# Time mixing of a two-layer encoder: chain and inverses as whole-array products with block-diagonal held operands

## The chip, the cores and the metric

The kernel runs on one core of a Trainium2 chip. A time is the device time of one execution in microseconds; a kernel's time is the median of its runs. All arithmetic is float32; the dense projections hold each operand as two rounded halves (`fp32r`) whose products are added.

## The reference

One sequence of 256 tokens, width 2048, 32 heads of 64, two layers. Layer 0 is RWKV-7 time mixing, layer 1 chunked attention; each is followed by a squared-ReLU MLP of width 8192, with norms and gates that a conditioning vector sets. The change touches the time mixing alone:

```python
def step(S, inp):                      # per head, S is 64 x 64, over 256 tokens
    r_t, w_t, k_t, v_t, kk_t, a_t = inp
    sa = jnp.einsum('bhvk,bhk->bhv', S, -kk_t)
    S = (S * w_t[:, :, None, :] + sa[..., None] * (kk_t * a_t)[:, :, None, :]
         + v_t[..., None] * k_t[:, :, None, :])
    y = jnp.einsum('bhvk,bhk->bhv', S, r_t)
    return S, y
...
y = ((y - mean) * lax.rsqrt(var + GN_EPS) * ln_w + ln_b)      # per head
y = y + jnp.sum(r_h * k_h * r_k, axis=-1, keepdims=True) * v_h
y = y.reshape(B, T, D).astype(h.dtype) * g
return y @ w_o
```

## The kernel before

The state is not stepped token by token. Tokens are taken in 4 chunks of 64; within a chunk the recurrence becomes matrix products with masked 64x64 Gram matrices and the inverse of a unit triangular one. Two heads form a pair, one on partitions 0 to 63, the other on 64 to 127; there are 16 pairs.

Each pair goes through four stages, and a software pipeline (`layer_a`) keeps one pair in each: the dense projections of `k` and `r` (`proj_steps`, 64 dense products at L405 and L406: 512 and 256 streamed columns), `early` (decays, norms, factors), `invert` and `late`. In each of 19 periods 16 slots are issued; in each slot some steps of `late`, `invert` and `early` and one part of the dense work. From this order a scheduler makes each engine's fixed queue. In the last three periods the output projection's first tiles (`o`, L394 to L396) take the dense part. In some slots a row of the conditioning weights is added up on VectorE (`acc`, L447), and its sums taken on TensorE (L469).

`invert` builds the Gram matrix of `bh` with `kr` (`gr`, L101), takes its diagonal 32x32 blocks, and inverts them by doubling: in each of 4 levels VectorE transposes `u` (L231), TensorE multiplies by the level's masked block (`iv<-tt,al`), ScalarE copies the result to `xs` (L235), TensorE multiplies `u` (`iv<-u,xs`) and VectorE adds (L246). A fifth level joins the two 32x32 halves (`co`). All these are 32x32 products in the array's four diagonal 32x32 tiles (`tiles`, L107): 16 for a level's half step, 4 chunks by 4 blocks. Masks of all levels are applied beforehand on GpSimd (`al`, L216).

`late` is the chain over the 4 chunks: for each, `g` (L273, L276), `sa` (L280), the state `zs` (L290, L292) and the output `py` (L283, L286, L301), each as two 64x64 products, one for each head, in the array's two diagonal 64x64 tiles. ScalarE copies `g` and `sa` out of PSUM, VectorE `zs`. The output is channel-major: its variance is a product of its squares with a block of ones (L111). Then come the gate's product (L315) and three operations on VectorE.

An f32 product is issued by the hardware as two passes, each with a load of its held operand, so it leaves two records under PE (the product) and two under PEld (the load).

Of the kernel before, what the change touches and what calls it, by code (L numbers as in the profile page):

```python
# [39 lines left out]
def _constants():  # L40
# [16 lines left out]
    for l in range(5):  # L57
        b = 1 << l
        m = ((i[:, None] // (2 * b) == i[None, :] // (2 * b))
             & (i[:, None] % (2 * b) >= b) & (i[None, :] % (2 * b) < b))  # L60
        put(f"lev{l}", np.tile(-m.T[:H, :H].astype(np.float32), (2, 1)))
    at["levs"] = (at["lev1"][0], 4 * H)
# [15 lines left out]
class Pair:  # L78
# [9 lines left out]
    def s(self, name="s", bufs=10):  # L88
        return self.b.pw.tile([P, T], F32, tag=name, bufs=bufs, name=name)

    def big(self, name, bufs):
        return self.b.pw.tile([P, 4, P], F32, tag=name, bufs=bufs, name=name)

    @staticmethod
    def ch(t):
        return t.rearrange("p (c t) -> p c t", t=C)
# [6 lines left out]
    def tiles(self, o, lhsT, rhs, pairs):  # L103

        for c in range(4):
            for R, K in pairs:
                self.b.nc.tensor.matmul(o[QS[K], c, :], lhsT[QS[R], c, :], rhs[QS[R], c, :], start=True, stop=True,  # L107
                                        tile_position=(H * R, H * K))
# [9 lines left out]
    def early(self):  # L118
# [37 lines left out]
        self.bh, self.kh = s("bh", 2), s("kh", 2)  # L156
# [8 lines left out]
        kr = self.kr = self.big("kr", 3)  # L165
        nc.vector.tensor_tensor(out=kr[:, :, 0:C], in0=ch(kk), in1=e0, op=ALU.mult)
        nc.vector.tensor_tensor(out=self.bh, in0=self.bh, in1=kk, op=ALU.mult)
        nc.vector.tensor_tensor(out=kr[:, :, C:P], in0=ch(r), in1=e1, op=ALU.mult)
# [3 lines left out]
        yield  # L172


        bk = self.bk = pw.tile([P, 3, 4, C], F32, tag="bk", bufs=3, name="bk")
        pt = b.psm().rearrange("p (a c k) -> p a c k", a=2, c=4)
        self.each(lambda c: pt[:, 0, c, :], lambda c: ch(v)[:, c, :], lambda c: cst("cen"))
        nc.scalar.copy(bk[:, 2], pt[:, 0])
        yield
        pbn = b.psm()[:, :T]  # L180
# [4 lines left out]
    def invert(self):  # L185
        b, nc, s, ch, kr, bk, bh, kh = self.b, self.b.nc, self.s, self.ch, self.kr, self.bk, self.bh, self.kh
        cst, pp = b.cst, b.pp

        def every(name):
            return cst(name).unsqueeze(1).to_broadcast([P, 4, H])  # L190

        def half(name, bufs):
            return b.pw.tile([P, 4, H], F32, tag=name, bufs=bufs, name=name)


        ui = cst("ui").unsqueeze(1).to_broadcast([P, 4, P])
        ts = []
        for src in (bh, kh):
            t = s()
            nc.gpsimd.tensor_tensor(out=ch(t), in0=ch(src), in1=self.pc.to_broadcast([P, 4, C]), op=ALU.mult)  # L200
            ts.append(t)
        pg = pp.tile([P, 4, P], F32, tag="gr", bufs=1, name="gr")
        self.each(lambda c: pg[:, c, :], lambda c: ch(bh)[:, c, :], lambda c: kr[:, c, :])
        ar = self.ar = s("ar", 2)
        nc.vector.tensor_tensor(out=ch(ar), in0=pg[:, :, C:P], in1=ui[:, :, C:P], op=ALU.mult)


        da, co, u = half("da", 2), half("co", 2), half("u", 2)
        for i, K in enumerate(QS):
            n = H * (i % 2)  # L210
            nc.scalar.copy(da[K], pg[K, :, n:n + H])
            if i % 2 == 0:
                nc.scalar.mul(co[K], pg[K, :, H:C], -1.0)
        nc.gpsimd.tensor_tensor(out=u, in0=da, in1=every("lev0"), op=ALU.mult)
        als = b.pw.tile([P, 4, 4, H], F32, tag="al", bufs=2, name="al")
        nc.gpsimd.tensor_tensor(out=als, in0=da.unsqueeze(1).to_broadcast([P, 4, 4, H]),  # L216
                                in1=cst("levs").rearrange("p (l k) -> p l k", l=4).unsqueeze(2).to_broadcast([P, 4, 4, H]),
                                op=ALU.mult)
        yield
        nc.vector.tensor_tensor(out=u, in0=u, in1=every("eye_h"), op=ALU.add)  # L220
# [4 lines left out]
        nc.scalar.copy(bk[:, 0:2], pt)  # L225
        yield
        uf = self.u = b.uf[self.j % 2]
        down, up = ((0, 1), (2, 3)), ((1, 0), (3, 2))
        for l in range(1, 6):
            tt_, xs = half("tt", 1), half("xs", 1)  # L230
            nc.vector.transpose(out=tt_.rearrange("p c t -> p (c t)"), in_=u.rearrange("p c t -> p (c t)"))  # L231
            pi = pp.tile([P, 16, H], F32, tag="iv", bufs=1, name="iv")[:, 0:4, :]
            if l < 5:
                self.tiles(pi, als[:, l - 1], tt_, [(i, i) for i in range(4)])
                nc.scalar.copy(xs, pi)  # L235
            else:
                self.tiles(pi, co, tt_, down)
                for i, K in enumerate(QS):
                    if i % 2:
                        nc.scalar.copy(xs[K], pi[K])  # L240
                    nc.gpsimd.tensor_copy(uf[K, :, H * (i % 2):H * (i % 2) + H], u[K])
            yield
            pi = pp.tile([P, 16, H], F32, tag="iv", bufs=1, name="iv")[:, 0:4, :]
            if l < 5:
                self.tiles(pi, xs, u, [(i, i) for i in range(4)])
                nc.vector.tensor_tensor(out=u, in0=u, in1=pi, op=ALU.add)  # L246
            else:
                self.tiles(pi, xs, u, up)
                for K in QS[::2]:
                    nc.vector.tensor_copy(uf[K, :, H:C], pi[K])  # L250
            if l == 2:
                pg = pp.tile([P, 4, P], F32, tag="gr", bufs=1, name="gr")
                self.each(lambda c: pg[:, c, :], lambda c: ch(kh)[:, c, :], lambda c: kr[:, c, :])
                mk = self.mk = self.big("mk", 2)
                nc.vector.tensor_tensor(out=mk, in0=pg, in1=ui, op=ALU.mult)
            yield

    def late(self):
        b, nc, j, s, ch, v = self.b, self.b.nc, self.j, self.s, self.ch, self.v
        kr, ar, mk, bk, u, pc, heads = self.kr, self.ar, self.mk, self.bk, self.u, self.pc, self.heads  # L260
        pw, pp = b.pw, b.pp

        pyt = pp.tile([P, 2, T], F32, tag="py", bufs=1, name="py")
        py = pyt[:, 0, :]
        zs = None
        for c in range(4):
# [5 lines left out]
            for K in heads:  # L272
                nc.tensor.matmul(pch[K, 0, :], mk[K, c, 0:C], bk[K, 2, c, :], start=True, stop=(c == 0))  # L273
            if c:
                for K in heads:
                    nc.tensor.matmul(pch[K, 0, :], kr[K, c, 0:C], zs[K, :], start=False, stop=True)  # L276
            nc.scalar.copy(g, pch[:, 0, :])
            yield
            for K in heads:
                nc.tensor.matmul(pch[K, 1, :], u[K, c, :], g[K, :], start=True, stop=True)  # L280
            nc.scalar.mul(sa, pch[:, 1, :], -1.0)
            for K in heads:
                nc.tensor.matmul(ch(py)[K, c, :], bk[K, 2, c, :], mk[K, c, C:P], start=True, stop=False)  # L283
            if c:
                for K in heads:
# [908 lines left out]
```

## Time and profile before

| | us |
|---|---|
| median of 3 runs | 2711.76 (2709.57 to 2712.15) |
| the profiled execution's own time | 2709.18 |
| its span, first to last instruction | 2707.4 |
| of it, the time mixing's pipeline | 210 to 750 |
| TensorE busy in these 540 us | 532.2 |
| VectorE, ScalarE, GpSimd busy there | 442.0, 270.2, 134.5 |

In a row of the profile "L107 PE MATMUL iv<-u,xs 32\*32 32x32 f32 x32" is line, engine, operation, output and operands by the program's names, the part of the array that is used (rows\*columns), the streamed operand (partitions x columns) and the number of records. In a timeline the first two numbers are start and length in microseconds. TensorE's products overlap: the length goes to the end of the last result, so what one costs is read from the distance between starts.

### The profile page before, as it was taken

How to read it: one execution, taken by the hardware profiler on the slowest of the kernel's cores; microseconds unless marked ns; L12 is line 12 of the kernel's file. 1: busy time of each engine (PE TensorE's matmuls, PEld its weight loads, DVE VectorE, ACT ScalarE, POOL GpSimd, SP SyncE). 2: the span in 40 equal slices, each digit the busy share in tenths (PEclk: the TensorE clock that was granted, in tenths of full speed). 3: DMA queues.
4: the chain of work that ended last, by engine and by line, in shares of the span. 5: the costliest groups of instructions: out<-in, count | busy, mean ns of one | idle time of the engine just before them, and what ended most of it. 6: DMA issues, size and time to landing. Idle time of an engine off the chain costs nothing.

```text
span 2707.4 us, 58382 instructions
## 1 busy us (share of the span) xinstructions
PE 2645.1 (98%) x23690; PEld 2236.3 (83%) x23690; DVE 2104.9 (78%) x3109; ACT 1347.8 (50%) x2432; POOL 214.9 (8%) x320
## 2 busy tenths in 40 slices
PE   6999999999999999999999999999999999999997
PEld 3777777777888888888888898877898888888886
DVE  5778888888788788888888898899987555555555
ACT  3346444555355536445355554465565464453553
POOL 0002222322110000000000100000100000000002
PEclk9999999999999999999999999999999999999999
DMA  9966655665587789988889769887867555555553
GB/s 338 313 227 207 203 191 180 191 195 177 184 280 264 255 324 329 330 307 319 322 316 329 252 220 316 322 287 252 288 193 259 188 188 186 187 188 186 189 188 120
DMA packets 217390, 662.64 MB, mean 245 GB/s; under 512 B 21408, under 2 KB 68896, under 8 KB 217120
## 3 DMA queue, kind: packets, MB, share of 16 engines
q1 hardware_dynamic: 215056, 656.36, 71.7%
q8 instruction: 186, 3.05, 0.4%
q10 hardware_dynamic: 2064, 2.54, 0.3%
q14 instruction: 84, 0.69, 0.1%
HBM read 656.72 MB, written 2.10 MB: 243 GB/s over the span
## 4 chain that ended last, share of the span: by engine, by line
PE 91%; DVE 3%; issue 3%; ACT 1%; DMA 1%; POOL 1%; DVEq 0%; ACTq 0%; SPq 0%; POOLq 0%
PE pj L405 47%; PE pj L406 23%; PE iv L107 2%; PE pj L395 2%; PE pj L396 2%; PE pj L394 2%; PE gr L101 1%; PE o L394 1%; PE ms L101 1%; PE chn L273 1%; PE chn L280 1%; PE ms L111 1%; PE py L315 1%; DVE wL L374 1%; PE o L395 0%
## 5 line engine op out<-in xcount | busy, mean ns | idle before, releaser
L374 DVE TENSOR_TENSOR wL<-raw,wH 128x1024 fp32r<-128x1024 f32 x772 | 941.8, 1220 | 353.5 <-ACT wH L371 348.8
L405 PE MATMUL pj<-aHL,wH 128*128 128x512 f32 x3328 | 1214.3, 405 | 2.0 <-DVE x L914 1.1
L371 ACT CAST wH<-raw 128x1024 fp32r<-128x1024 f32 x772 | 805.9, 1045 | 796.6 <-PE pj L405 650.4
L406 PE MATMUL pj<-aHL,wL 128*128 128x256 f32 x3328 | 938.8, 282 | 0.0
L405 PEld LDWEIGHTS pj<-aHL,wH 128*128 128x128 f32 x3328 | 628.0, 189 | 154.4 <-issue 11.4
L405 PE MATMUL pj<-hHL,wH 128*128 128x512 f32 x2048 | 722.4, 398 | 0.0
L406 PEld LDWEIGHTS pj<-aHL,wL 128*128 128x128 f32 x3328 | 628.3, 189 | 3.9 <-issue 0.8
L406 PE MATMUL pj<-hHL,wL 128*128 128x256 f32 x2048 | 574.4, 281 | 0.0
L405 PEld LDWEIGHTS pj<-hHL,wH 128*128 128x128 f32 x2048 | 384.5, 188 | 93.8 <-DVE hHL L960 0.2
L406 PEld LDWEIGHTS pj<-hHL,wL 128*128 128x128 f32 x2048 | 386.8, 189 | 0.5 <-DVE wL L374 0.3
L447 DVE SCALAR_TENSOR_TENSOR acc<-rada,ct,acc 128x1024 f32<-128x1024 f32 x255 | 326.3, 1280 | 11.7 <-DMA rada<-w_ada 11.1
L511 POOL TENSOR_TENSOR ss<-ss,sq 128x256 f32<-128x256 f32 x56 | 54.8, 979 | 1587.1 <-ACT sq L510 1586.9
L985 DVE SCALAR_TENSOR_TENSOR x<-pj,mod,x 128x256 f32<-128x256 f32 x256 | 123.4, 482 | 58.4 <-PE pj L406 54.6
L447 DVE SCALAR_TENSOR_TENSOR acc<-raw,ct,acc 128x1024 f32<-128x1024 f32 x105 | 135.6, 1291 | 3.8 <-DMA raw<-w_ada 3.7
L396 PE MATMUL pj<-aHL,wL 128*128 128x258 f32 x384 | 108.6, 283 | 1.6 <-DVE wL L374 1.6
L957 ACT ACTIVATE t<-t 128x256 f32<-128x256 f32 x112 | 46.8, 418 | 126.9 <-DVE t L929 126.9
L395 PE MATMUL pj<-aHL,wH 128*128 128x258 f32 x384 | 109.6, 286 | 0.0
L394 PE MATMUL pj<-aHL,wH 128*128 128x258 f32 x384 | 109.5, 285 | 0.0
L396 PEld LDWEIGHTS pj<-aHL,wL 128*128 128x128 f32 x384 | 73.9, 193 | 1.9 <-DVE wL L374 1.8
L395 PEld LDWEIGHTS pj<-aHL,wH 128*128 128x128 f32 x384 | 73.3, 191 | 0.1
L394 PEld LDWEIGHTS pj<-aHL,wH 128*128 128x128 f32 x384 | 73.0, 190 | 0.2
L959 ACT ACTIVATE t<-t 128x256 f32<-128x256 f32 x128 | 53.4, 417 | 3.4
(244 smaller groups left out, 2846.6 us busy)
## 6 DMA issues: line engine op xcount, KB each, us to landing
raw<-w_up SPq DMA_DIRECT2D x256, 512.0 KB, 4.3
raw<-w_down SPq DMA_DIRECT2D x256, 512.0 KB, 4.2
rada<-w_ada SPq DMA_DIRECT2D x208, 512.0 KB, 5.7
raw<-w_ada SPq DMA_DIRECT2D x112, 512.0 KB, 4.4
rawa<-w_ada SPq DMA_DIRECT2D x64, 512.0 KB, 6.7
rada<-w_ada_kv SPq DMA_DIRECT2D x64, 512.0 KB, 6.2
raw<-w_k SPq DMA_DIRECT2D x32, 512.0 KB, 4.7
raw<-w_r SPq DMA_DIRECT2D x32, 512.0 KB, 4.7
```

What stands on the lines that cost most here:

```text
L101: self.b.nc.tensor.matmul(o(c)[K], lhsT(c)[K], rhs(c)[K], start=True, stop=True)
L107: self.b.nc.tensor.matmul(o[QS[K], c, :], lhsT[QS[R], c, :], rhs[QS[R], c, :], start=True, stop=True, tile_position=(H * R, H * K))
L371: nc.scalar.copy(Hf, raw)
L374: eng.tensor_tensor(out=Lf, in0=raw, in1=Hf, op=ALU.subtract)
L394: nc.tensor.matmul(ps, H[:, i, :], a(kt)[:, 0, :], start=(first and kt == 0), stop=False)
L395: nc.tensor.matmul(ps, H[:, i, :], a(kt)[:, 1, :], start=False, stop=False)
L396: ins = nc.tensor.matmul(ps, L[:, i, :], a(kt)[:, 0, :], start=False, stop=(last and kt == KT - 1))
L405: nc.tensor.matmul(ps, H[:, i, :], a(kt), start=(kt == 0), stop=False)
L406: ins = nc.tensor.matmul(ps[:, 0, :], L[:, i, :], a(kt)[:, 0, :], start=False, stop=(kt == KT - 1))
L447: nc.vector.scalar_tensor_tensor(out=self.acc, in0=raw, scalar=ck, in1=self.acc, op0=ALU.mult, op1=ALU.add)
L511: (eng or nc.gpsimd).tensor_tensor(out=self.ss, in0=self.ss, in1=sq, op=ALU.add)
L985: nc.vector.scalar_tensor_tensor(out=x, in0=ps[:, i, :], scalar=self.mods[(layer, 5)][:, n:n + 1], in1=x, op0=ALU.mult, op1=ALU.add)
```

## The change

The 32x32 and 64x64 products of inverses and chain become products of the whole 128x128 array. Their held operands are 128x128 matrices with the heads' (or quarters') blocks on the diagonal and zeros elsewhere. These operands (`kr`, `nega`, `co`, `xs`, `xc`, `ar`, `uf`, `bk`, `mk`) live in buffers that are zeroed once and whose diagonal blocks alone are written: a copy or product into such a buffer is now one instruction for each head or quarter. Most of them have one buffer. `nega` holds the whole negative block; a level's mask is applied when the result is taken into `u`, by a predicated copy on VectorE. The sign is put into `bh`. The chain's output becomes token-major: squares are summed along the row on VectorE, the normed output `yn` is transposed back by TensorE with `eye`. The two transpositions of `bh` and `kh`, and the Gram matrix of `kh`, stand at the end of `invert` (12 steps in place of 13). The inverses' products go through the new function `whole`; transpositions and Gram matrices stay 64x64 products.

```diff
-    def tiles(self, o, lhsT, rhs, pairs):
+    @staticmethod
+    def of(h, t):
+        K = slice(C * h, C * h + C)
+        return t[K][..., K]
+
+    def whole(self, o, lhsT, rhs):
         for c in range(4):
-            for R, K in pairs:
-                self.b.nc.tensor.matmul(o[QS[K], c, :], lhsT[QS[R], c, :], rhs[QS[R], c, :], start=True, stop=True,
-                                        tile_position=(H * R, H * K))
+            self.b.nc.tensor.matmul(o[:, c, :], lhsT[:, c, :], rhs[:, c, :], start=True, stop=True)
...
-        kr = self.kr = self.big("kr", 3)
-        nc.vector.tensor_tensor(out=kr[:, :, 0:C], in0=ch(kk), in1=e0, op=ALU.mult)
-        nc.vector.tensor_tensor(out=kr[:, :, C:P], in0=ch(r), in1=e1, op=ALU.mult)
+        kr = self.kr = b.kr[j % 2]
+        for part, src, e in ((0, kk, e0), (1, r, e1)):
+            for h, K in enumerate(self.heads):
+                nc.vector.tensor_tensor(out=self.of(h, kr)[:, :, part, :], in0=ch(src)[K], in1=e[K], op=ALU.mult)
...
         for i, K in enumerate(QS):
             n = H * (i % 2)
-            nc.scalar.copy(da[K], pg[K, :, n:n + H])
+            nc.vector.copy_predicated(u[K], flips("lev0", K), pg[K, :, n:n + H])
+            nc.scalar.copy(nega[K, :, K], pg[K, :, n:n + H])
...
         for l in range(1, 6):
...
             if l < 5:
-                self.tiles(pi, als[:, l - 1], tt_, [(i, i) for i in range(4)])
-                nc.scalar.copy(xs, pi)
+                self.whole(pi, nega, tt_)
+                for K in QS:
+                    nc.scalar.copy(xs[K, :, K], pi[K])
             else:
-                self.tiles(pi, co, tt_, down)
+                self.whole(pi, co, tt_)
+                for i in (0, 2):
+                    nc.scalar.copy(xc[QS[i + 1], :, QS[i]], pi[QS[i + 1]])
...
             if l < 5:
-                self.tiles(pi, xs, u, [(i, i) for i in range(4)])
-                nc.vector.tensor_tensor(out=u, in0=u, in1=pi, op=ALU.add)
+                self.whole(pi, xs, u)
+                nc.vector.copy_predicated(u, flips(f"lev{l}"), pi)
             else:
-                self.tiles(pi, xs, u, up)
+                self.whole(pi, xc, u)
...
-            for K in heads:
-                nc.tensor.matmul(pch[K, 1, :], u[K, c, :], g[K, :], start=True, stop=True)
-            nc.scalar.mul(sa, pch[:, 1, :], -1.0)
-            for K in heads:
-                nc.tensor.matmul(ch(py)[K, c, :], bk[K, 2, c, :], mk[K, c, C:P], start=True, stop=False)
+            mm(pch[:, 1, :], u[:, c, :], g, start=True, stop=True)
+            nc.scalar.copy(sa, pch[:, 1, :])
+            mm(py[:, c, :], mk[:, c, 1, :], bv[:, c, :], start=True, stop=False)
...
-        self.head_sums(var, sq)
+        nc.vector.tensor_reduce(out=rg, in_=ch(sq), axis=AX.X, op=ALU.add)
...
+        nc.vector.tensor_tensor(out=yn, in0=py, in1=rg.unsqueeze(2).to_broadcast([P, 4, C]), op=ALU.mult)
+        yield
+        self.each(lambda c: yf[:, c, :], lambda c: yn[:, c, :], lambda c: b.cst("eye"))
...
+            def spread(name, *shape):
+                t = pw.tile([P, *shape, P], F32, name=name)
+                nc.gpsimd.memset(t, 0.0)
+                return t
+
+            self.kr = [spread(f"kr_{i}", 4, 2) for i in range(2)]
+            self.nega, self.co, self.xs, self.xc = (spread(n_, 4) for n_ in ("nega", "co", "xs", "xc"))
+            self.ar = [spread(f"ar_{i}", 4) for i in range(2)]
+            self.uf, self.bk, self.mk = spread("uf", 4), spread("bk", 2, 4), spread("mk", 4, 2)
```

In the changed kernel the dense lines 405 and 406 are 411 and 412, the inverses' products are L108, the grams L203, other 64x64 products L97, the chain's L285 to L306. How the change moves TensorE's queue is shown at two places. The first is one level of an inverse in the steady state; a shape here is the output's, so 32x32 is one tile and 128x32 the whole array. Before:

```order
L107 MATMUL iv<-tt,al 32x32 x16
L273 MATMUL chn<-bk,mk 64x64
L276 MATMUL chn<-zs,kr 64x64 x2
L405 MATMUL pj<-aHL,wH 128x512
L406 MATMUL pj<-aHL,wL 128x256
L405 MATMUL pj<-aHL,wH 128x512
L107 MATMUL iv<-u,xs 32x32 x16
```

With the change, one level in the steady state:

```order
L108 MATMUL iv<-tt,nega 128x32 x4
L411 MATMUL pj<-aHL,wH 128x512
L412 MATMUL pj<-aHL,wL 128x256
L411 MATMUL pj<-aHL,wH 128x512
L412 MATMUL pj<-aHL,wL 128x256
L203 MATMUL gr<-kr_2235,kh 64x128 x2
L108 MATMUL iv<-u,xs 128x32 x4
```

Sixteen products become four, and two of the eight products of the Gram matrix of `kh` have moved between the two halves of the step, where the chain's small products stood.

The second place is the chain on TensorE. Before, `g` is used, the state formed, and dense products follow each group:

```order
L280 MATMUL chn<-g,uf_2235 64x64 x2
L286 MATMUL py<-kr,zs 64x64 x2
L405 MATMUL pj<-aHL,wH 128x512
L406 MATMUL pj<-aHL,wL 128x256
L405 MATMUL pj<-aHL,wH 128x512
L406 MATMUL pj<-aHL,wL 128x256
L290 MATMUL chn<-bk 64x64 x2
L292 MATMUL chn<-sa,bk 64x64 x2
L301 MATMUL py<-ar,sa 64x64 x2
```

With the change, in the second chunk of the same kind of period:

```order
L292 MATMUL py<-bv,mk 128x64
L111 MATMUL ms<-sq,csts 128x256
L285 MATMUL chn<-bv,mk 128x64
L287 MATMUL chn<-zs,kr_2237 128x64
L294 MATMUL py<-zs,kr_2237 128x64
L290 MATMUL chn<-g,uf 128x64
L297 MATMUL chn<-bv,bk 128x64
L298 MATMUL chn<-sa,bk 128x64
L306 MATMUL py<-sa,ar_2249 128x64
```

Here a chunk's whole chain stands in one piece with no dense product in it; in its other chunks dense products stand between the groups as before. On ScalarE the copy after an inverse's product was one and is now four, with casts of weight halves between them. Before:

```order
L235 COPY xs<-iv 128x128
L277 COPY g<-chn 128x64
L371 CAST wH<-raw 128x1024
L281 ACTIVATE sa<-chn 128x64
L151 ACTIVATE s<-s 128x256
```

With the change:

```order
L239 COPY xs<-iv 32x4x32 x4
L848 COPY k<-pj 128x256
L377 CAST wH<-raw 128x1024
L288 COPY g<-chn 128x64
L291 COPY sa<-chn 128x64
```

Four quarter copies stand where one whole one stood, and the casts are queued between such groups in both.

More of the change, by code (lines that the diff above doesn't have):

```diff
@@ new lines, in half, with flips, gram @@
+        def half(name):
+            return b.pw.tile([P, 4, H], F32, tag=name, bufs=1, name=name)
+        def flips(name, K=slice(None)):
+            return every(name, K).bitcast(mybir.dt.uint32)
+        def gram(t):
+            pg = pp.tile([P, 4, P], F32, tag="gr", bufs=1, name="gr")
+            for c in range(4):
+                for h, K in enumerate(self.heads):
+                    nc.tensor.matmul(pg[K, c, :].rearrange("p (a t) -> p a t", t=C), ch(t)[K, c, :],
+                                     self.of(h, kr)[:, c, :, :], start=True, stop=True)
+            return pg
```

160 lines of the change are left out of this document (70 added, 90 removed).

## The prediction

> **What bounds the kernel now.** I read the page first, then the busy time of the stretch in which the changed code runs, then what TensorE waits for there, and last its timeline.
>
> ```profile
> span 2707.4 us, 58382 instructions
> PE 2645.1 (98%) x23690; PEld 2236.3 (83%) x23690; DVE 2104.9 (78%) x3109; ACT 1347.8 (50%) x2432; POOL 214.9 (8%) x320
> PE 91%; DVE 3%; issue 3%; ACT 1%; DMA 1%; POOL 1%; DVEq 0%; ACTq 0%; SPq 0%; POOLq 0%
> ```
>
> TensorE holds 91% of the chain that ended last. The time mixing's pipeline runs from 210 to 750 us. Its windows view, for all instructions and then for the tiles `iv` (inverses), `chn` and `py` (chain) alone:
>
> ```profile
> 210.00:750.00 540.00, 532.16 (x9638) 414.19 (x9639) 441.96 (x807) 270.22 (x732) 134.48 (x178) 1.00 0.60 190
> 210.00:750.00 540.00, 72.38 (x4608) 54.80 (x4608) 27.08 (x96) 25.05 (x96) 1.00 0.60 190
> 210.00:750.00 540.00, 74.12 (x1088) 48.38 (x1088) 12.05 (x48) 27.82 (x128) 1.00 0.60 190
> 210.00:750.00 540.00, 73.63 (x800) 48.87 (x800) 14.14 (x32) 13.72 (x32) 1.00 0.60 190
> PE iv L107 <- DVE tt L231: 2.2, 4, 0.6
> PE py L301 <- issue: 1.0, 1, 1.0
> ```
>
> TensorE is busy for 532.2 of 540 us at full clock (1.00), and its longest wait (last two rows, from the waits of PE) is 2.2 us over four occasions. No other engine is above 82%. So what the change does to TensorE's own work in these 540 us is what it does to the kernel. But "busy" has overlapping instructions in it, so the price of one is read from starts, one behind the other:
>
> ```profile
> 422.39 0.28 PE L406 MATMUL pj<-aHL,wL 128*128 128x256 f32 x1
> 422.52 0.40 PE L405 MATMUL pj<-aHL,wH 128*128 128x512 f32 x1
> 422.75 0.28 PE L406 MATMUL pj<-aHL,wL 128*128 128x256 f32 x1
> 422.96 0.33 PE L290 MATMUL chn<-bk 64*64 64x64 f32 x4
> 423.12 0.28 PE L292 MATMUL chn<-sa,bk 64*64 64x64 f32 x4
> 423.24 0.28 PE L301 MATMUL py<-ar,sa 64*64 64x64 f32 x4
> 423.45 0.51 PE L405 MATMUL pj<-aHL,wH 128*128 128x512 f32 x1
> 423.80 0.28 PE L406 MATMUL pj<-aHL,wL 128*128 128x256 f32 x1
> 432.74 0.45 PE L107 MATMUL iv<-u,xs 32*32 32x32 f32 x32
> 433.12 0.39 PE L406 MATMUL pj<-aHL,wL 128*128 128x256 f32 x1
> ```
>
> Three prices stand here. **Dense**: L405 takes 0.23 us and L406 0.12 to 0.13. **A visit to small tiles**: L406 takes 0.21 when a 64*64 product is next (0.09 more), the last small group 0.21 where the one ahead of it took 0.12 (0.09 more), and the first L405 afterwards 0.35 (0.11 more). That is 0.29 us a visit, 0.145 for each change of tile size. **Small products**: an f32 product makes two records (a pass each), so x4 is one pair of heads, 0.12 us; and 32 passes of 32*32, four side by side, take 0.38 with the 0.09 of leaving, so 0.29.
>
> **The change on TensorE.** What each whole product costs is not in the trace: a 128x128 held operand with only 32 or 64 streamed columns. Its held operand must be loaded, and the loads have rows of their own (PEld):
>
> ```profile
> 422.06 0.19 PEld L405 LDWEIGHTS pj<-aHL,wH 128*128 128x128 f32 x1
> 422.16 0.19 PEld L406 LDWEIGHTS pj<-aHL,wL 128*128 128x128 f32 x1
> 422.96 0.20 PEld L290 LDWEIGHTS chn<-bk 64*64 64x64 f32 x4 [0.25 <-ACT bk L225]
> 423.07 0.20 PEld L292 LDWEIGHTS chn<-sa,bk 64*64 64x64 f32 x4
> 423.45 0.19 PEld L405 LDWEIGHTS pj<-aHL,wH 128*128 128x128 f32 x1
> 423.56 0.19 PEld L406 LDWEIGHTS pj<-aHL,wL 128*128 128x128 f32 x1
> ```
>
> After a visit nothing is loaded ahead, and L406's load begins 0.10 to 0.11 us behind L405's: a load of 128 columns holds the loader that long, and the 0.11 that the first L405 loses is the same load seen from the products. Four loads of 64 columns, two side by side, take 0.11, so 0.055 each: the time goes with the columns. In the dense stream the load hides behind 256 streamed columns (0.12). Behind 32 or 64 it cannot: an f32 pass streams 64 columns in 0.06 (x4 in 0.12 above). So a whole pass costs 0.10 at the least if loads follow one another without a gap, 0.12 at the most if it goes like L406, whose load and stream are each about as long; if a load cost nothing it would be 0.058. I take 0.11, the loads' own distance.
>
> Counted in the two programs' orders, over 16 pairs:
>
> - Added: 640 inverse products (10 steps of 4 a pair) and 448 chain products (28 a pair), two passes each: 2176 × 0.11 = 239.4 us.
> - Removed, inverses: 2304 products, 4608 passes, 144 groups of 32 × 0.29 = 41.8 us.
> - Removed, chain: 896 products, 448 pairs of heads × 0.12 = 53.8 us.
> - Norm of the output: the head sums of `sq` go (16 products of 256 columns, 0.43 each, 6.9 us), and a transposition of `yn` comes (64 pairs of heads × 0.12 = 7.7 us). The price of 0.43 is from these rows: L315's four passes take 0.68 to the next dense start, which is itself 0.18 late (0.30 against 0.12), 0.215 a pass:
>
> ```profile
> 448.18 0.40 PE L405 MATMUL pj<-aHL,wH 128*128 128x512 f32 x1
> 448.41 1.03 PE L315 MATMUL py<-tg,lg 128*128 128x256 f32 x4
> 449.09 0.47 PE L406 MATMUL pj<-aHL,wL 128*128 128x256 f32 x1
> 449.39 0.40 PE L405 MATMUL pj<-aHL,wH 128*128 128x512 f32 x1
> ```
>
> - Changes of tile size: 709 in the section before, 319 after; 390 × 0.145 = 56.6 us saved. It isn't more because the grams, the two transpositions by `eye` and `cen`, the new one and the sums of `acc` stay small, and the gram of `kh` is now issued in 59 pieces where it was in 25.
>
> Work: 239.4 − 41.8 − 53.8 − 6.9 + 7.7 = +144.6; with the changes saved, **+88 us**.
>
> [...]
>
> **The change beside TensorE.**
>
> ```profile
> 442.04 0.45 PE L107 MATMUL iv<-tt,al 32*32 32x32 f32 x32
> 442.42 0.51 PE L405 MATMUL pj<-aHL,wH 128*128 128x512 f32 x1
> 442.62 0.27 ACT L235 COPY xs<-iv 128x128 f32<-128x128 f32 x1 [0.16 <-PE iv L107]
> 443.34 0.45 PE L107 MATMUL iv<-u,xs 32*32 32x32 f32 x32
> L371 ACT CAST wH<-raw 128x1024 fp32r<-128x1024 f32 x772 | 805.9, 1045 | 796.6 <-PE pj L405 650.4
> L211 ACT COPY da<-gr 32x128 f32<-32x128 f32 x64 | 16.3, 255 | 10.8 <-DVE ar L205 10.2
> L246 DVE TENSOR_TENSOR u<-u,iv 128x128 f32<-128x128 f32 x64 | 18.0, 282 | 17.2 <-PE iv L107 16.6
> ```
>
> The copy of `xs` becomes four copies of one 32-row quarter each. A copy of 32x128 takes 0.255 (L211), so ScalarE is done 0.20 + 4 × 0.255 = 1.22 us after the product's last start slot, where it was 0.47 (442.89 against 442.42). In the new order two to three dense pairs and a gram piece stand between the two products of a step, 0.7 to 1.2 us; the second product is then 0.0 to 0.5 late, on 64 steps: at 0.2 each, 13 us. Queued behind it are the dense products, which wait too. In a quarter of the chain's steps only two whole passes stand between a product and the one that needs its copy (0.22 us against about 0.5 for latency and copy): some 4 us. Against this, fewer TensorE instructions are to be fetched ("issue" waits of 1 us, as above), and the loads slow the pace, which gives every copy more room. I take +12, bounds 0 and 30.
>
> Hidden, each by TensorE's own time: VectorE's extra halves of `kr`, `ar` and `mk` and the new `yn` and sum, less the pieces that go (some 1.5 us a pair on 442 of 540, which becomes 466 of about 640); the predicated copies stand for the additions into `u`, 0.28 (L246), and I bound them by twice that; ScalarE's extra copies (12 of 0.255 for `xs`, and a few more: about 4 us a pair, 334 of 640). If that cover were gone, they would cost at most 24 and 64 us. The zeroing of the held buffers, 7680 elements, falls on GpSimd ahead of its first use:
>
> ```profile
> 217.14 0.56 POOL L817 MEMSET uf<- 128x256 f32 x2 [29.43 <-DVE aHL L564]
> 227.02 0.93 POOL L147 COPY pc<-e 128x4 f32<-128x4 f32 x1 [9.31 <-ACT e L143]
> ```
>
> 512 elements take 0.56, so 8.4 us, from 217.1 to 225.5: within the 9.3 us that GpSimd waits here. Uncovered it would cost 8 once. Single buffers (`r`, `bh`, `uf`, `bk`, `mk`, `e01`) are written after the last reader in the order of issue; I give them nothing. DMAs are unchanged.
>
> **Sum.** The profiled execution took 2709.2 us (span 2707.4). 2709.2 + 88 + 12 = 2809; the median of the runs is 2.6 above that execution, so **2812 us**.
>
> **The rivals.**
>
> *Loads hidden: faster.* The place is the whole products; the mechanism, that the next operand is loaded while the present one streams and several loads are under way at once, as for small tiles. Then a pass costs its stream, 0.058: 2176 × 0.058 = 126.2, work +31.4, less 56.6, so −25: 2687. It decides from a pass under about 0.07, where 2176 passes cost no more than what goes. For it: before the dense products loads do run ahead. Against it: the loads at 422.06 and 423.45 follow one another at 0.10 and 0.11, never closer, in one and the same tile. [...]
>
> *Starved by the copies: slower still.* A cast of a weight half (L371, 1.05 us on ScalarE) is queued ahead of the four copies in half of the 64 steps, and the second product waits for it: 32 × 1.05 = 34 us beyond the forecast, 2846. For it: casts and copies alternate in ScalarE's order. Against: the row above shows TensorE waiting hardly at all on `xs` now.
>
> *The change does less than it says.* If whole f32 products between dense ones also cost 0.145 a change, nothing is saved: 2869. Against it: L405 at 448.18 is followed by the whole product L315 after 0.23, its usual time.
>
> **How the numbers follow.** Forecast 0.76; starved 0.12; hidden loads 0.07; changes not saved 0.01; passes half hidden, near 0.08 us, 0.04 (2712 + 88 − 2176 × 0.03 = 2735). Low end: passes at 0.105 and no new wait give 2712 + 77 = 2789, and I go down to 2772 towards the half hidden ones. High end: passes at 0.12 and 30 of waits give 2712 + 110 + 30 = 2852, cut to 2848. A change of this kernel can be told from none at about 0.2%, 5 us. Faster 0.07, same 0.02, slower 0.91.
>
> **What would show it.** In the changed kernel's timeline a group of four `iv` products (x8) should take 0.88 us to the next start, and loads within it follow at 0.11; L405 after such a group should take its 0.23, not 0.35. The section should end about 100 us later, with TensorE still busy at 97% or more and its waits for ScalarE's `xs` near 10 us in total. Loads closer than 0.07, or TensorE idle for tens of us, would make the prediction wrong.

## The result: slower by 6.7%, about twice the loss forecast

| | us |
|---|---|
| before, median of 4 runs | 2711.95 (2709.57 to 2712.62) |
| changed, median of 4 runs | 2919.01 (2888.01 to 2943.24) |
| changed, the two faster runs | 2888.01 and 2897.94 |
| ratio of those to before | 1.0669, 95% interval 1.0636 to 1.0702 |
| the profiled execution shown here | 2943.24, span 2941.4 |

The forecast was 2812, from 2772 to 2848. The executions differ with the clock that each was granted (a mean of 0.971, 0.967, 0.951 and 0.947 at 2888.01, 2897.94, 2940.07 and 2943.24 us), so the ratios here and below are taken from the faster ones, while the profile below shows the slowest.

The page of the changed kernel: span, busy times, granted clock in 40 slices, and the chain that ended last.

```profile
span 2941.4 us, 50764 instructions
PE 2867.0 (97%) x19690; PEld 2480.4 (84%) x19690; DVE 2135.0 (73%) x3188; ACT 1417.3 (48%) x2688; POOL 173.4 (6%) x313
PEclk9998689966797999999999999999999999999999
PE 88%; DVE 4%; issue 3%; ACT 2%; DMA 2%; SPq 0%; POOL 0%; DVEq 0%; ACTq 0%; POOLq 0%
```

TensorE is busy for 97% (98% before) and holds the chain. What is new is the third row: between the 4th and the 13th slice the granted clock falls to 0.6 to 0.9. The time mixing ends at 980 us, not at 750. The windows view of that stretch, for all instructions, then for the tiles `iv`, `chn` and `py`, and then in four pieces (columns as in the prediction; the clock is the number after the five engines):

```profile
212.00:980.00 768.00, 748.56 (x5575) 656.37 (x5574) 473.62 (x884) 339.45 (x987) 91.97 (x171) 0.82 0.43 133
212.00:980.00 768.00, 210.17 (x1280) 203.02 (x1280) 19.34 (x64) 82.01 (x320) 0.82 0.43 133
212.00:980.00 768.00, 98.08 (x544) 87.34 (x544) 8.95 (x32) 30.58 (x144) 0.82 0.43 133
212.00:980.00 768.00, 101.14 (x672) 80.76 (x672) 22.08 (x48) 6.14 (x16) 0.82 0.43 133
300.00:400.00 100.00, 97.18 (x709) 85.35 (x707) 58.97 (x111) 42.80 (x125) 9.28 (x20) 0.78 0.40 123
700.00:800.00 100.00, 97.62 (x632) 84.36 (x628) 52.61 (x100) 36.21 (x106) 9.45 (x20) 0.69 0.36 113
800.00:900.00 100.00, 98.08 (x871) 86.34 (x869) 71.41 (x142) 56.87 (x175) 13.02 (x23) 1.00 0.44 138
1000.00:1500.00 500.00, 495.30 (x3280) 436.00 (x3279) 426.24 (x519) 252.09 (x376) 7.25 (x8) 1.00 0.87 306
```

At 0.69 to 0.78 TensorE is as busy (97 to 98 of 100 us) as at 1.00, but gets through 632 to 709 records in 100 us, not 871 (the mix of the work differs too; the prices below don't hang on it). In the section as a whole the mean is 0.82, where it was 1.00. Behind it, from 1000 to 1500 us, the mean is 1.00. Inside these sections the two traces' own records of the clock hold only the values 1.0 and 0.5, each for a whole number of steps of 3.41 us (one step at 1.0 from 342.2, 15 at 0.5 from 704.1); added up, the section spends 273 of its 768 us at half clock, against 3 of 540 before.

What half clock does stands in two stretches of TensorE's timeline (start, length). At full clock:

```profile
824.90 0.60 PE L111 MATMUL ms<-rkp,csts 128*128 128x256 f32 x2
825.34 0.97 PE L108 MATMUL iv<-tt,nega 128*128 128x32 f32 x8
826.15 0.48 PE L411 MATMUL pj<-aHL,wH 128*128 128x512 f32 x1
826.47 0.28 PE L412 MATMUL pj<-aHL,wL 128*128 128x256 f32 x1
826.58 0.40 PE L411 MATMUL pj<-aHL,wH 128*128 128x512 f32 x1
826.82 0.28 PE L412 MATMUL pj<-aHL,wL 128*128 128x256 f32 x1
827.55 1.08 PE L108 MATMUL iv<-u,xs 128*128 128x32 f32 x8 [0.45 <-ACT xs L239]
828.47 0.48 PE L411 MATMUL pj<-aHL,wH 128*128 128x512 f32 x1
828.79 0.28 PE L412 MATMUL pj<-aHL,wL 128*128 128x256 f32 x1
```

At half clock:

```profile
708.89 0.63 PE L411 MATMUL pj<-aHL,wH 128*128 128x512 f32 x1
709.32 1.75 PE L108 MATMUL iv<-tt,nega 128*128 128x32 f32 x8
710.88 0.56 PE L412 MATMUL pj<-aHL,wL 128*128 128x256 f32 x1
711.24 0.63 PE L411 MATMUL pj<-aHL,wH 128*128 128x512 f32 x1
711.67 0.41 PE L412 MATMUL pj<-aHL,wL 128*128 128x256 f32 x1
711.88 0.63 PE L411 MATMUL pj<-aHL,wH 128*128 128x512 f32 x1
```

A group of eight `iv` passes takes 0.81 to 0.92 us to the next start at full clock (the forecast was 0.88) and 1.56 at half; L411 takes 0.24 and 0.43, L412 0.11 to 0.12 and 0.21. A product has two passes here too (1280 records for the 640 inverse products). Read from all starts, the median whole pass costs 112 ns at full clock, with 32 and with 64 streamed columns alike, and 213 ns at half. The second group above also waited 0.45 us for its `xs`, so waiting cannot be ruled out yet.

What TensorE waits for in the section (line, releaser, us in total, times, longest):

```profile
PE chn L297 <- ACT sa L291: 6.5, 10, 0.9
PE iv L108 <- DVE tt L234: 4.4, 4, 1.7
PE chn L290 <- ACT g L288: 3.1, 4, 0.9
PE iv L108 <- ACT xs L239: 2.8, 6, 0.8
```

TensorE's idle time in the section is 20.3 us, 8.4 before. That cannot make 200 us by itself. The difference between the sections, 768 − 540 = 228 us, has another source, and the experiments take it apart.

### The profile page after: what moved, and what is told of

It is laid out like the page before. It is cut to its first block, busy times and chain, and to the rows that moved or that the text cites. A ratio compares the mean times of both kernels' runs of the same rounds, so it can differ in the third digit from the quotient of the medians.

```text
span 2941.4 us, 50764 instructions
## 1 busy us (share of the span) xinstructions
PE 2867.0 (97%) x19690; PEld 2480.4 (84%) x19690; DVE 2135.0 (73%) x3188; ACT 1417.3 (48%) x2688; POOL 173.4 (6%) x313
## 4 chain that ended last, share of the span: by engine, by line
PE 88%; DVE 4%; issue 3%; ACT 2%; DMA 2%; SPq 0%; POOL 0%; DVEq 0%; ACTq 0%; POOLq 0%
PE pj L411 42%; PE pj L412 21%; PE iv L108 7%; PE gr L203 2%; PE pj L401 1%; PE pj L402 1%; PE pj L400 1%; PE ms L97 1%; DVE wL L380 1%; DVE acc L453 1%; PE o L400 1%; PE py L306 1%; DMA rada<-w_ada 1%; PE py L322 1%; PE chn L290 1%
## 5 line engine op out<-in xcount | busy, mean ns | idle before, releaser
L411 PE MATMUL pj<-aHL,wH 128*128 128x512 f32 x3328 | 1241.8, 413 | 2.0 <-DVE x L928 1.1
L412 PE MATMUL pj<-aHL,wL 128*128 128x256 f32 x3328 | 956.9, 288 | 0.1
L411 PEld LDWEIGHTS pj<-aHL,wH 128*128 128x128 f32 x3328 | 648.4, 195 | 150.6 <-issue 11.0
L411 PE MATMUL pj<-hHL,wH 128*128 128x512 f32 x2048 | 724.6, 399 | 0.0
L412 PEld LDWEIGHTS pj<-aHL,wL 128*128 128x128 f32 x3328 | 647.7, 195 | 3.0 <-issue 1.2
L412 PE MATMUL pj<-hHL,wL 128*128 128x256 f32 x2048 | 574.6, 281 | 0.0
L411 PEld LDWEIGHTS pj<-hHL,wH 128*128 128x128 f32 x2048 | 384.8, 188 | 95.9 <-DVE hHL L974 0.2
L412 PEld LDWEIGHTS pj<-hHL,wL 128*128 128x128 f32 x2048 | 386.8, 189 | 0.1
L453 DVE SCALAR_TENSOR_TENSOR acc<-rada,ct,acc 128x1024 f32<-128x1024 f32 x255 | 326.2, 1279 | 11.5 <-DMA rada<-w_ada 10.9
L250 DVE COPY_PREDICATED u<-csts,iv 128x128 f32<-128x128 uint32 x64 | 19.3, 302 | 186.7 <-PE iv L108 186.7
L453 DVE SCALAR_TENSOR_TENSOR acc<-raw,ct,acc 128x1024 f32<-128x1024 f32 x105 | 134.4, 1280 | 0.8
L239 ACT COPY xs<-iv 32x128 f32<-32x128 f32 x256 | 65.6, 256 | 110.1 <-PE iv L108 105.6
L971 ACT ACTIVATE t<-t 128x256 f32<-128x256 f32 x112 | 46.8, 418 | 126.9 <-DVE t L943 126.9
L108 PEld LDWEIGHTS iv<-u,xs 128*128 128x128 f32 x512 | 84.6, 248 | 13.9 <-ACT xs L239 9.2
L108 PEld LDWEIGHTS iv<-tt,nega 128*128 128x128 f32 x512 | 83.4, 241 | 11.7 <-issue 4.3
```

The source lines that it names most:

```text
L108: self.b.nc.tensor.matmul(o[:, c, :], lhsT[:, c, :], rhs[:, c, :], start=True, stop=True)
L239: nc.scalar.copy(xs[K, :, K], pi[K])
L411: nc.tensor.matmul(ps, H[:, i, :], a(kt), start=(kt == 0), stop=False)
L412: ins = nc.tensor.matmul(ps[:, 0, :], L[:, i, :], a(kt)[:, 0, :], start=False, stop=(kt == KT - 1))
L453: nc.vector.scalar_tensor_tensor(out=self.acc, in0=raw, scalar=ck, in1=self.acc, op0=ALU.mult, op1=ALU.add)
```

## Experiments

Two theories were to be told apart. **By the streaming**: the clock is halved because whole products with 32 or 64 streamed columns keep the array waiting on loads; TensorE counts as busy, but columns pass through it for only a quarter to a half of the time (an estimate: 32 or 64 columns in a pass of 112 ns, at 0.84 ns each, as L111's two passes of 256 columns start 215 ns apart). **By the copies**: the clock is halved because TensorE has to wait again and again for the four copies of `xs` and for `g` and `sa`. Beside these, the sum's terms were to be measured one by one. Every time is a median of 4 or 5 runs; "loss" is its distance from the kernel before as run beside it (2711.95 for the changed kernel; 2710.59 for wide_iv, wide_all, inv_tiles and chain_tiles; 2711.34 for both_tiles_one_copy; 2712.21 for the others). Section, half clock in it, and changes of tile size are added up from each trace, which is one execution. The section starts up to 2 us later in some kernels than in the one before, and that is taken off, so it can be 1 to 2 us shorter than the window shown.

| kernel | inverses | chain | us | loss | section | half clock | changes |
|---|---|---|---|---|---|---|---|
| before | 32x32 | 64x64 | 2711.95 | | 540 | 3 | 709 |
| changed | whole, 32 columns | whole, 64 | 2919.01 | 207 | 768 | 273 | 319 |
| wide_iv | whole, 128 | whole, 64 | 2809.27 | 98.7 | 636 | 3 | 272 |
| wide2_iv | whole, 64 | whole, 64 | 2833.15 | 120.9 | 659 | 48 | 289 |
| wide_all | whole, 128 | whole, 128 | 2816.93 | 106.3 | 641 | 3 | 176 |
| wide_iv_chain_tiles | whole, 128 | 64x64 | 2800.66 | 88.5 | 627 | 0 | 463 |
| chain_tiles | whole, 32 | 64x64 | 2897.48 | 186.9 | 721 | 184 | 458 |
| inv_tiles | 32x32 | whole, 64 | 2755.93 | 45.3 | 583 | 34 | 544 |
| inv_tiles_wide_chain | 32x32 | whole, 128 | 2735.49 | 23.3 | 566 | 7 | 476 |
| both_tiles | 32x32 | 64x64 | 2733.44 | 21.2 | 560 | 10 | 669 |
| both_tiles_one_copy | 32x32 | 64x64 | 2722.88 | 11.5 | 555 | 27 | 631 |

### More columns through the same held operand

Each inverse product streams all four chunks, 128 columns, and the result of its own chunk alone is used. Loads, copies and the number of products are those of the changed kernel.

```diff
-            self.b.nc.tensor.matmul(o[:, c, :], lhsT[:, c, :], rhs[:, c, :], start=True, stop=True)
+            self.b.nc.tensor.matmul(o[:, 4 * c:4 * c + 4, :], lhsT[:, c, :], rhs, start=True, stop=True)
...
+            pf = pp.tile([P, 16, H], F32, tag="iv", bufs=1, name="iv")
+            pi = pf[:, 0:16:5, :]
```

> Each inverse product streams all four chunks (128 columns) in place of one (32); the held operand, its load, the copies and the result used are the same, and the three quarters more of output are not read. Changes of tile size are 272 in this program's order (319 in the change). Theory 1 (the clock is halved when TensorE streams columns for too small a share of the time): a 128-column f32 pass streams for 0.107 us of the 0.112 that the load holds it, so it costs no more, and the granted clock in the time mixing comes back to 0.95 or more; time 2712 + 88 - 47 x 0.145 + 12 = about 2805, range 2790 to 2835 as the chain still streams 64. Theory 2 (the clock is halved because TensorE waits for the four copies of xs): the waits are untouched, so the clock stays near 0.82 there and the time stays between 2880 and 2940. If a pass costs load and stream one after the other, it would take 0.22 and the time would be some 140 us above the change.

Measured: 2809.27 us, ratio to before 1.0359 (1.0344 to 1.0375). Four times the columns make the kernel 110 us faster than the changed one by the medians, 84 by its two faster runs. The page's row of the clock, the section in the windows view, and the same groups in the timeline:

```profile
PEclk9999999999999999999999999999999999999999
```

```profile
210.00:848.00 638.00, 624.33 (x5645) 550.48 (x5645) 478.89 (x888) 343.24 (x990) 115.84 (x171) 1.00 0.52 161
```

```profile
595.09 1.16 PE L108 MATMUL iv<-tt,nega 128*128 128x128 f32 x8
596.01 0.48 PE L413 MATMUL pj<-aHL,wH 128*128 128x512 f32 x1
596.33 0.28 PE L414 MATMUL pj<-aHL,wL 128*128 128x256 f32 x1
597.53 1.16 PE L108 MATMUL iv<-u,xs 128*128 128x128 f32 x8 [0.21 <-ACT xs L240]
598.45 0.48 PE L413 MATMUL pj<-aHL,wH 128*128 128x512 f32 x1
```

A group takes 0.92 to the next start with 128 columns (595.09 to 596.01), as with 32 at full clock (827.55 to 828.47): the 96 columns more cost it nothing. The clock stays at 1.00, though the copies are the same in number and TensorE waits longer for `xs` than in the changed kernel, 5.3 us against 2.8:

```profile
PE iv L108 <- ACT xs L240: 5.3, 20, 0.6
PE chn L299 <- ACT sa L293: 1.4, 5, 0.4
```

So the copies of `xs` are not the cause, and neither are the zeros in the held operands, which are the same too. The waits for `g` and `sa` are not untouched, though: with 0.2 us for `g` they come to 1.6 us, against 9.6 in the changed kernel, in the order that the scheduler built for this kernel. This run alone does not rule them out. One wait that both kernels have helps to tell: at the first inverse TensorE idles for 1.72 us, and a shorter wait for `xs` follows. In the changed kernel, then in wide_iv, the first product behind the wait, and the whole step of the clock's records (3.41 us) in which this happens:

```profile
244.26 1.05 PE L108 MATMUL iv<-tt,nega 128*128 128x32 f32 x8 [1.72 <-DVE tt L234]
243.30:246.70 3.40, 2.04 (x14) 1.70 (x14) 2.82 (x5) 2.94 (x11) 1.65 (x3) 1.00 0.70 169
```

```profile
243.19 1.13 PE L108 MATMUL iv<-tt,nega 128*128 128x128 f32 x8 [1.72 <-DVE tt L234]
241.30:244.70 3.40, 1.68 (x18) 1.53 (x14) 3.28 (x7) 3.29 (x10) 0.94 (x2) 1.00 0.70 218
```

In the changed kernel half clock follows, from 246.7 us on. In wide_iv, where TensorE is busy for even less of the step (1.68 us, not 2.04) but with wide products, the clock holds. This is the kernel that the forecast described: 98.7 us slower, where the sum said 100 (93 with this kernel's 272 changes of tile size).

The same edit with the chunk streamed only twice (64 columns) shows a size between:

```diff
+            self.b.nc.tensor.matmul(o[:, 2 * c:2 * c + 2, :], lhsT[:, c, :],
+                                    rhs[:, c, :].unsqueeze(1).to_broadcast([P, 2, H]), start=True, stop=True)
...
+            pi = pf[:, 0:8:2, :]
```

> As wide_iv, but each inverse product streams its chunk twice (64 columns, not 128). 289 changes of tile size. A pass still costs its load, 0.112 us, of which columns stream for 0.053, as in the chain. If the clock goes by the share of time in which columns stream, it is held nearly as well as with 128: half clock under 60 us in the time mixing (273 in the change's profiled execution, 3 with 128 columns), time 2805 to 2840. If it goes by something that 128 columns brought in another way (a different order of instructions), 64 need not help: over 2850.

Measured: 2833.15 us, ratio 1.0445 (1.0429 to 1.0460), 48 us of half clock:

```profile
210.00:870.00 660.00, 647.03 (x5577) 568.39 (x5575) 477.44 (x885) 342.39 (x988) 106.26 (x171) 0.96 0.50 155
```

32, 64 and 128 columns give 273, 48 and 3 us of half clock with the same products and loads. Both the number of drops to half clock and their length fall: 13 drops of 21 us on average, 5 of 9.6, and one of 3.4. The chain can be widened as well, by streaming its operand twice:

```diff
+            two = lambda t: t.unsqueeze(1).to_broadcast([P, 2, C])
...
-                mm(pch[:, 0, :], kr[:, c, 0, :], zs, start=False, stop=True)
+                mm(pch[:, 0], kr[:, c, 0, :], two(zs), start=False, stop=True)
```

(and so for every product of the chain)

> As wide_iv, and the chain's products too stream 128 columns (the operand twice; the second copy is not read). 176 changes of tile size. Theory 1: hardly any half clock is left in the time mixing (under 20 us), time 2712 + 88 - 143 x 0.145 + 12 = about 2791, range 2775 to 2810. Theory 2: as the change, 2880 to 2940.

Measured: 2816.93 us, ratio 1.0388 (1.0373 to 1.0404). With the inverses wide there is no half clock left to win back (3 us in both), and the wider chain is 7.7 us slower than wide_iv: TensorE idles for 25.2 us, not 14.0. The gain that had been expected did not come.

### One part alone

The inverses go back into the array's 32x32 tiles, out of the same zeroed buffers; the chain stays whole.

```diff
+            for R, K in pairs:
+                self.b.nc.tensor.matmul(o[QS[K], c, :], lhsT[QS[R], c, QS[K]], rhs[QS[R], c, :], start=True, stop=True,
+                                        tile_position=(H * R, H * K))
```

> The change with its inverses' products put back into the four 32x32 tiles (2304 products); chain whole, all copies and buffers as in the change. 544 changes of tile size. By the prices: chain 896 passes x 0.112 - 53.8 + 0.8 for the norm - 165 x 0.145 = +23.5 us, so 2736 at full clock. Theory 1: the chain's passes stream 0.053 of 0.112 us, and the clock holds most of the time: 2730 to 2765. Theory 2: the four copies of xs are still there and halve the clock: over 2800.

Or the chain goes back into two 64x64 tiles, and the inverses stay whole:

```diff
+        def hm(o, lhsT, rhs, **kw):
+            for K in self.heads:
+                mm(o[K], lhsT[K][..., K], rhs[K], **kw)
...
-            mm(pch[:, 1, :], u[:, c, :], g, start=True, stop=True)
+            hm(pch[:, 1, :], u[:, c, :], g, start=True, stop=True)
```

> The change with its chain's products put back into the two 64x64 tiles; inverses whole. 458 changes of tile size. By the prices: 1280 passes x 0.112 - 41.8 + 0.8 - 251 x 0.145 = +66 us and 12 of waits, 2790 at full clock. Theory 1: the inverses' passes stream only 0.027 of 0.112 us, the clock is still halved for 100 us or more in the time mixing, and the time is 2840 to 2890. Theory 2: as theory 1 here, since the copies are the same; this run tells which part has the cost, not which theory.

Measured: 2755.93 us with the inverses back, ratio 1.0176 (1.0151 to 1.0200); 2897.48 us with the chain back, ratio 1.0650 (1.0593 to 1.0707). The sections of the two, inverses back first:

```profile
210.00:794.00 584.00, 564.93 (x8901) 474.29 (x8902) 474.42 (x885) 342.81 (x988) 117.03 (x171) 0.97 0.57 176
```

```profile
210.00:932.00 722.00, 693.51 (x6471) 577.02 (x6470) 474.07 (x885) 341.03 (x988) 96.11 (x171) 0.87 0.46 142
```

The kernel with the inverses back came in the range of theory 1, and the one with the chain back 7 us above its range. The whole inverses make most of the loss and most of the half clock (184 us without the whole chain, 34 without the whole inverses). Whether the two together cost more half clock (273) than added up (218) is not shown: these are single executions, and the changed kernel's mean clock went from 0.947 to 0.971 over its runs.

With both back, everything else of the change is left: spread buffers, quarter copies, predicated copies, the norm by rows, the new order.

> The change with all its products, inverses and chain, put back into the small tiles; what is left of the change are the block-diagonal buffers, the four copies of xs, the predicated copies, the token-major output and the later Gram matrix of kh. 669 changes of tile size (709 before). If loads and clock are the whole cost of the change: 2712 + 0.8 - 40 x 0.145 = 2707, and up to 15 us of waits for copies, so 2700 to 2725, at full clock. If the copies, the halves on VectorE or the single buffers cost of themselves, as a rival has it: 2740 or more.

Measured: 2733.44 us, ratio 1.0081 (1.0065 to 1.0098). So the rest of the change costs 21.2 us, some 8 more than the highest that was expected. Two combinations give the steps between, each with one product kind whole and 128 columns wide:

> Inverses whole with 128 streamed columns, chain in the two 64x64 tiles: the cost of the whole inverses alone, without the clock. 463 changes of tile size. 1280 x 0.112 - 41.8 + 0.8 - 246 x 0.145 = +66.7 and 12 of waits: 2790, range 2775 to 2805, half clock under 20 us. With 32 columns the same kernel took 2897.

> Inverses in the four 32x32 tiles, chain whole with 128 streamed columns (the operand twice): the cost of the whole chain alone, without the clock. 476 changes of tile size. 896 x 0.112 - 53.8 + 0.8 - 233 x 0.145 = +13.6: 2726, with waits up to 2745. With 64 columns it took 2756 and had 34 us of half clock in the time mixing; if the share of streamed columns is the cause, under 10 us are left; else they stay.

Measured: 2800.66 us, ratio 1.0326 (1.0311 to 1.0342), and 2735.49 us, ratio 1.0087 (1.0072 to 1.0102). The clock in their sections is 1.00 and 0.99. So at full clock the steps from before to wide_iv can be read one after the other: the rest +21, whole inverses +67 (88.5 − 21.2), whole chain +10 (98.7 − 88.5). With the inverses in tiles, a wide whole chain costs only 2 us more than the 64x64 one, which the intervals do not tell from nothing.

### Where the rest's 21 us lie

As both_tiles, but one copy takes `xs` out into a contiguous tile, as before the change:

```diff
-                for K in QS:
-                    nc.scalar.copy(xs[K, :, K], pi[K])
+                x1 = half("x1")
+                nc.scalar.copy(x1, pi)
```

> As both_tiles (all products back in small tiles, the rest of the change kept), but the product of an inverse's half step is again taken out by one copy into one contiguous tile, not by four copies of a 32-row quarter each. Where do the 21 us between before and both_tiles come from? Theory A, the order: the chain stands in one piece, so its products wait for g and sa (7.9 us of waits in both_tiles against 0.2 before); the copies cost only their waits of 3.2 us and little else, and this run is at 2728 to 2734. Theory B, the copies: twelve more instructions a pair on ScalarE delay everything behind them, g and sa too; then this run is at 2724 or below and the waits for g and sa fall with it.

Measured: 2722.88 us, ratio 1.0040 (1.0025 to 1.0054): 10.6 us less than both_tiles. TensorE's waits for `g`, `sa` and `xs` in the section of both_tiles, of this kernel (where `x` is the new tile), and of the kernel before:

```profile
PE chn L282 <- ACT g L294: 5.5, 7, 1.6
PE iv L109 <- ACT xs L241: 3.2, 9, 0.6
PE chn L282 <- ACT sa L297: 1.9, 6, 0.4
```

```profile
PE chn L282 <- ACT g L294: 9.4, 13, 1.7
PE chn L282 <- ACT sa L297: 2.8, 10, 0.4
PE iv L109 <- ACT x L241: 0.5, 1, 0.5
```

```profile
PE chn L290 <- ACT sa L281: 0.2, 1, 0.2
PE iv L107 <- ACT xs L235: 0.2, 1, 0.2
```

The time is the one of theory B, 2724 or below, but not by its way: the waits for `g` and `sa` did not fall, they rose from 7.4 to 12.2 us, so the copies of `xs` do not make those. The wait for `xs` fell by 2.7 us, and the scheduler, with twelve instructions a pair fewer on ScalarE, built another order with 38 fewer changes of tile size. The waits hold little of the 10.6 us: TensorE's idle time in the section falls from 22.7 to 21.0 us, and the half clock, which cost 0.49 us for each us of it between wide_iv and the changed kernel, is longer here (27 us, not 10). What the order gave is not settled further. Of all the kernels run, none is faster than the one before.

## Why the prediction was right in kind and wrong in size

**The failed step** is in "What bounds the kernel now": "TensorE is busy for 532.2 of 540 us at full clock (1.00)", and from it "what the change does to TensorE's own work in these 540 us is what it does to the kernel". The clock was read as a property of the section, and every price in the sum, "2176 × 0.11" above all, was taken at it. The change itself takes it away: a whole pass costs 112 ns at 1.0 and 213 at 0.5, and the dense products slow with it (L411 from 0.24 to 0.43 us). Between wide_iv and the changed kernel the section grows by 132 us (636 to 768) for 270 us more half clock, 0.49 us for each. No rival and no bound contained this, so the range ended 40 us below the fastest run.

**The sum itself holds where the clock does.** Term by term:

| term | forecast | measured |
|---|---|---|
| a whole pass, loads not hidden | 0.11 us | 0.112 us with 32 or 64 columns; eight in 0.92 with 128, as with 32 |
| all whole inverses for tiles | +69 (140.8 − 41.8, less 206 changes × 0.145) | +67 |
| the whole chain for tiles | +17 (98.6 − 53.8, less 191 × 0.145) | +10 (+2 with inverses in tiles) |
| the rest | +7 (0.8 of the norm, 12 of waits, less 40 × 0.145) | +21 |
| sum at full clock | +93 with wide_iv's 272 changes (+100 with 319) | +98.7 (wide_iv) |
| half clock | 0 | +84 (faster runs) to +110 (median) |

In the forecast's column the changes of tile size are those of the kernels that the runs compare, so its terms add up to 93; the changed kernel has 319, as counted beforehand, and with these the sum is the recorded 100. The total agrees partly by luck: the rest was 14 us dearer than priced, and the chain some 7 cheaper.

**The single signs.** "A group of four `iv` products (x8) should take 0.88 us": 0.81 to 0.92 at full clock. "L405 after such a group should take its 0.23, not 0.35": it takes 0.32 (826.15 to 826.47), and the same behind a wide group (596.01 to 596.33), so 0.09 of the 0.11 that L405 lost after a visit remains behind a whole group, and a group does not give back all that a visit cost. "The section should end about 100 us later": 97 in wide_iv, 230 in the changed kernel. "TensorE still busy at 97% or more": 97%, and this is what misled, since TensorE was as busy at a mean clock of 0.69 to 0.78 (97 to 98 of 100 us). "Its waits for ScalarE's `xs` near 10 us": 2.8; TensorE's idle time did grow by 12 us (20.3 − 8.4), as forecast, but most of the growth stands at the chain's `g` and `sa` (9.6), the place that was given 4.

The loads of the group at full clock, from the view of the load engine:

```profile
825.12 1.07 PEld L108 LDWEIGHTS iv<-tt,nega 128*128 128x128 f32 x8
826.12 0.19 PEld L411 LDWEIGHTS pj<-aHL,wH 128*128 128x128 f32 x1
826.23 0.19 PEld L412 LDWEIGHTS pj<-aHL,wL 128*128 128x128 f32 x1
```

Eight loads take 1.00 us to the next one's start. In the single records the first is pulled ahead by 0.21 us, and the others and L411's follow at 0.11; L412's begins 0.11 behind L411's, none closer: the passes (0.112) stand as far apart as their loads, as forecast.

**The rivals.** *Loads hidden* (2687) is refuted by the pass of 112 ns, and so is *passes half hidden* (2735). *Starved by the copies* (2846) is refuted: 2.8 us of waits for `xs` where it asked for 34 more. *Changes not saved* (2869) came nearest in time, and the 0.09 us left behind each `iv` group is a part of it, but the totals at full clock leave no room for 57 us.

## What to carry to other kernels

Before pricing a change in which TensorE's products become narrow, work out for what share of the time columns stream through the array, not only how long TensorE is busy, and look at the stretches of a few microseconds in which it also waits. In these traces each of the 50 drops to half clock followed a step with a share of at most 0.41, and of some 1720 steps at full clock above that none was followed by one: where a change brings the share near it, price both clocks (a whole pass cost 112 ns at one and 213 at the other). Where a product waited for its own load anyway, streaming more columns through it held the clock here (3 us of half clock with 128 columns, 273 with 32); 128 columns for 32 cost the inverses' groups nothing (0.92 us either way), while widening the chain gained 20 us with the inverses in tiles (2755.93 to 2735.49) and cost 7.7 with the inverses already wide. And small tiles were the cheaper form here: four 32x32 products side by side beat one whole product with a block-diagonal operand by 67 us in 160 half steps (at full clock), in spite of the changes of tile size.

## What the runs showed of the hardware that was not expected

The granted clock was halved while TensorE was busy for 97% of the changed kernel's section and nowhere idle for longer than 1.72 us. To see what goes with it, each step of 3.41 us of the clock's records in the time mixing of all eleven traces was given a share: the time in which columns stream, each product weighted by the rows of the array that it uses, at 0.83 ns a column for an f32 pass (L111's two passes of 256 columns start 215 ns apart, 0.84 a column) and half of that for fp32r (L411's 512 columns take 427 ns at half clock, 0.83 a column, so 0.42 at full), divided by the step. The shares are estimates from these times.

| | steps | share of the time streaming |
|---|---|---|
| full clock, next step at half | 50 | at most 0.41 |
| full clock below 0.40, next step at full | 12 | 0.33 to 0.40 |
| full clock above 0.41, next step at half | 0 of some 1720 | |
| half clock, next step at full | 50 | 0.34 or more, median 0.41 |
| half clock, next step at half | 124 | at most 0.41 |

How a product that straddles two steps is counted moves single shares, and so these bounds, by some 0.03. The kernel before has two steps below 0.40 and dropped after one of them; the changed kernel has 15 and dropped after 13. The mean of 97% hides that waits go with this: 12 of those 13 steps contain a wait of TensorE, most often for the chain's `g` and `sa`, and TensorE is busy in those 12 for 0.46 to 0.91 of the time. But idle time alone does not decide here. The step of wide_iv shown above is busy for 1.68 of 3.40 us, has a share of 0.40 and is followed by full clock. This one, of chain_tiles, has no idle time and a share of 0.34, and half clock follows it:

```profile
338.80:342.20 3.40, 3.40 (x86) 3.05 (x86) 0.46 (x2) 1.24 (x5) 0.00 (x0) 1.00 0.55 159
```

And both_tiles_one_copy, with 12.2 us of waits for `g` and `sa` but small tiles, has 27 us of half clock, not 273. No run kept the narrow whole products and took away the waits, so how much half clock the narrow products would bring by themselves is open.

A step at half clock was followed by another one 124 times and by full clock 50 times. By the same estimate a 32-column pass of 213 ns streams for 0.027 us of full-speed time, a share of 0.13, where the same pass at full clock has 0.24; the drops are longest (21 us on average) in the changed kernel, and that this low share is what prolongs them was not shown. The bound of about 0.40 is taken from ten of these traces; in the eleventh (both_tiles_one_copy) all five drops followed shares of 0.27 to 0.36. It belongs to these kernels, and whether rows are weighted rightly was not tried by a run of its own.

The longest idle time of TensorE in the changed kernel's section, 1.72 us, is about half a step of the clock's records, so none of its 13 drops came behind a step without work. The changed kernel against wide_iv, with 32 or 128 columns streamed through the same operands (273 and 3 us of half clock), shows what went with the drops: a small share of streaming, from narrow products with short waits or, as in the step of chain_tiles, without.
